# A hybrid encoder trunk: branch pieces go on TensorE only in every second gap between dense products

## The chip, the cores and the metric

The kernel runs on one core of a Trainium2 chip. The metric is the device time of one execution in microseconds; the median of three runs of the kernel before is 1067.63 us.

## What is computed

Two layers of an encoder over 256 tokens of width 1024, all in float32, and a last RMSNorm. Each layer projects the normalised tokens once and feeds four branches from it, merges them through sigmoid gates, and ends with a SwiGLU block. Cut to what matters:

```
h = rms_norm(x); proj = h @ w_in                    # 1024 -> 10000 columns
aq ak av ao ag | bq bk bv | cq ck cv | dq dk dv | gl = split(proj)
y_a = bidirectional mLSTM (4 heads of 128, centred short convolution on q, k)
y_b = grouped-query attention (8 heads of 64, 2 kv heads, rotary)
y_c = neighbourhood attention (8 heads of 64, 8 x 16 window, relative bias)
y_d = softmax(q1 k1' + alibi) v - lambda * softmax(q2 k2' + alibi) v     # 4 heads
merged = sum_g sigmoid(gl_g) * (y_g @ w_up_g);  x += merged @ w_out
h2 = rms_norm(x);  x += (silu(h2 @ w_gate) * (h2 @ w_up)) @ w_down       # 1024 -> 2816 -> 1024
```

## The kernel before

**Dense products.** A float32 product is made of three products of rounded halves, hi x hi, hi x lo and lo x hi (`mm3`, line 354). A weight tile comes by DMA into one of four `raw` buffers; ScalarE (ACT) writes the high half `whi` (`emit_hi`, 255), VectorE (DVE) the low half `wlo` = raw - whi (`emit_lo`, 262), five buffers each. The activations stand as `xT` or `yt`, halves too. Every engine call goes through one line (166), so that the profile's line is the same everywhere, and the tile names tell the work apart: `pd` are the three PSUM banks of the dense products, used in turn (`bank`, 333), `pa` the five banks of the branches.

**What sets the order.** The kernel is a list scheduler written out in the program: the order in which `trunk` issues is the order in each engine's queue. It walks through blocks of dense products (`PLAN`, line 32 and following: d0 d1 dv bkv a0 a1 av bq and so on; then `wo` and the SwiGLU). A block of 512 columns (`blk512`, 368) issues runs of 6 or 12 wide products (128x512), `bkv` (1158) runs of 12 narrow ones (128x272), 6 into `pd1` and 6 into `pd2`. Between two runs it calls `slot` (293): a gap. In each gap, in this order: the evacuations that are due (`later`, 320: the one of a finished bank is issued one gap later), one `emit_lo` on even gaps and one `emit_hi` on odd ones (both if the weights are behind), and then one step of each branch task that is ready.

**The pieces.** The branches are generators: `a_gates`, `a_head`, `soft_item` (one pair of heads of b, c or d), `soft_tail`, `y_up` and others. They run up to their next `yield` in one gap. A piece is a step that puts work on TensorE: transposes (`pa<-ident,...`), score products of 64 rows (`pa<-rq`, 12 of them per item, the two heads in the two halves of the rows), products with the values (`pa<-vd,w` and `pa<-re,...`). A piece starts with a loop that waits for free banks and buffers, as `while not (PS.ok(1) and RE.ok(1)): yield` (917). Between the pieces of an item lie steps without TensorE. In `soft_item` for d these are: the score step on DVE (four `CUSTOM_DVE_ANT_0` with the ALiBi distance, out `w2` and `sm`), four exps on ACT, the normalisation on DVE (a `RECIPROCAL`, then products and sums into `w`), the transposes, a copy, the products with `vd`, a copy into `k4`, two squares on ACT. A product with `vd` or a transpose of `w` is float32 throughout; the products with `vd` stand in the trace as two records each. A step is taken only when by the planner's own durations its operands are ready (`step`, 278).

**The place behind `bkv`.** `bkv` fills `pd1` and `pd2`. Their evacuation `done` (1162) is, for each: `gtok` on DVE, `ktok` and `vb` (high half) on ACT, `vb` (low half) on DVE. It is issued one gap behind the block. The next block `a0` puts its first 6 wide products into `pd0` and the next 6 into `pd1`.

Of the kernel before, what the change touches and what calls it, by code (L numbers as in the profile page):

```python
# [170 lines left out]
def trunk(ctx: ExitStack, tc, x_in, wts, par, parc, cst, dist, t2w, fg, out):  # L171
# [15 lines left out]
    PS = Res([psp.tile([128, 512], F32, name="pa%d" % i, tag="pa%d" % i) for i in range(5)])  # L187
# [9 lines left out]
    RQ = many(2, "rq_", [128, 2, 512], F32R)  # L197
    RE = many(3, "re_", [128, 2, 512], F32R)
# [6 lines left out]
    K4 = many(4, "k4_", [128, 1024])  # L205
    W2 = many(8, "w2_", [128, 512])
# [5 lines left out]
    SM = many(8, "sm_", [128, 16])  # L212
# [17 lines left out]
    with tc.manual_schedule():  # L230

        tasks, urgent, pending = [], [], []
        state = {"load": 0, "hi": 0, "lo": 0, "bank": 0, "u": 0, "live": 0, "n": 0, "dma": 1.5}
        nhalf = 2 * L * NU

        consts = []
# [39 lines left out]
        ready = {}  # L276
# [16 lines left out]
        def slot(forced=False):  # L293

            for r in everyres:
                r.flush()
            now = [p for p in pending if p[0] <= 0]
            pending[:] = [(p[0] - 1, p[1]) for p in pending if p[0] > 0]
            for _, f in now:
                f()  # L300

            if state["u"] <= 2:
                step(urgent, forced)
            if not forced:
                state["n"] += 1
                behind = state["hi"] - state["live"] < NH - 1
                if state["n"] % 2 == 0 or behind:
                    emit_lo()
                if state["n"] % 2 == 1 or behind:
                    emit_hi()  # L310
            if state["u"] > 2:
                step(urgent, forced)
            step(tasks, forced)
# [246 lines left out]
        def y_up(b, y):  # L560
            while not yt_ok(b):
                yield
            yt = yt_get(b)
            for t in (0, 1):
                while not PS.ok(1):
                    yield
                p = PS.get()
                for k in range(4):
                    T.transpose(p[:, k * 128:(k + 1) * 128], y[:, t, k * 128:(k + 1) * 128], ident)
                yield  # L570
                p4 = p.rearrange("p (k n) -> p k n", k=4)
                A.activation(yt[:, 0, :, tsl(t)], p4, AF.Copy)
                yield
                sub_lo(yt[:, 1, :, tsl(t)], p4, yt[:, 0, :, tsl(t)])
                PS.put(p)
            yield
            Bs[b]["yt"] = yt


        def a_gates(res):  # L580

            while not W2.ok(3):
                yield
            w0, w1, w2 = W2.get(), W2.get(), W2.get()
            g = gtok
            g4 = g.rearrange("p (n k h) -> p n k h", k=2, h=4)
            f = w1[:, 32:48]
            V.tensor_copy(f.rearrange("p (n h) -> p n h", h=4), g4[:, :, 1, :])
            for d in (0, 1):
                V.tensor_copy(iz[:, :, 32 * d:32 * d + 4],  # L590
                              g.rearrange("p (t d k h) -> p t d k h", t=2, d=2, k=2)[:, :, d, 0, :])
            mn, ab = w1[:, 48:64], w1[:, 64:80]
            V.tensor_scalar(mn, f, 0.0, None, op0=ALU.min)
            yield
            A.activation(ab, f, AF.Abs)
            A.activation(ab, ab, AF.Exp, scale=-1.0)
            yield
            z, q, pl = w1[:, 80:96], w1[:, 96:112], w1[:, 112:128]
            V.tensor_scalar(z, ab, 2.0, None, op0=ALU.add)
            V.reciprocal(z, z)  # L600
            V.tensor_tensor(z, z, ab, op=ALU.mult)
            V.tensor_tensor(q, z, z, op=ALU.mult)
            V.tensor_scalar(pl, q, 1.0 / 17.0, None, op0=ALU.mult)
            yield
            for n in (15, 13, 11, 9, 7, 5, 3):
                V.scalar_tensor_tensor(pl, pl, 1.0 / n, q, op0=ALU.add, op1=ALU.mult)
                if n == 9:
                    yield
            V.scalar_tensor_tensor(pl, pl, 1.0, z, op0=ALU.add, op1=ALU.mult)
            G.memset(w2[0:36, 0:512], 0.0)  # L610
            G.memset(w0[0:36, 0:512], 0.0)
            yield
            lf = w1[:, 128:144]
            V.scalar_tensor_tensor(lf, pl, -2.0, mn, op0=ALU.mult, op1=ALU.add)
            lf4 = lf.rearrange("p (t d h) -> p t d h", t=2, d=2)
            for d in (0, 1):
                V.tensor_copy(rowz[:, :, d, 32 * d:32 * d + 4], lf4[:, :, d, :])
            yield
            while not PS.ok(1):
                yield  # L620
            p = PS.get()
            tri = cs[:, K_TRI:K_TRI + 384]
            T.matmul(p[0:36, 0:256], rowz[:, 0, 0, :], tri[:, 0:256], start=True, stop=False)
            T.matmul(p[0:36, 0:256], rowz[:, 1, 1, :], tri[:, 128:384], start=False, stop=False)
            T.matmul(p[0:36, 128:256], rowz[:, 1, 0, :], tri[:, 0:128], start=False, stop=False)
            T.matmul(p[0:36, 0:128], rowz[:, 0, 1, :], tri[:, 256:384], start=False, stop=True)
            for t in (0, 1):
                T.transpose(p[0:36, 256 + 128 * t:384 + 128 * t], iz[:, t, :], ident)
            yield

            ar, br = w1[0:36, 0:256], w1[0:36, 256:512]
            A.activation(br, p[0:36, 0:256], AF.Copy)
            yield
            V.tensor_tensor(ar, p[0:36, 256:512], br, op=ALU.subtract)
            PS.put(p)
            V.tensor_scalar(w2[0:36, 128:384], ar, 0.0, None, op0=ALU.max)
            a_, b_ = w2, w0
            for i in range(8):
                d = 1 << i
                V.tensor_tensor(b_[0:4, 128:384], a_[0:4, 128:384], a_[0:4, 128 - d:384 - d], op=ALU.max)  # L640
                V.tensor_tensor(b_[32:36, 128:384], a_[32:36, 128:384], a_[32:36, 128 + d:384 + d], op=ALU.max)
                a_, b_ = b_, a_
                if i % 2 == 1:
                    yield
            m = a_[0:36, 128:384]
            V.tensor_tensor(br, br, m, op=ALU.add)
            A.activation(mrow[0:36, 0, :], m, AF.Copy)
            yield
            A.activation(br, br, AF.Exp, scale=-1.0)
            sub_lo(mrow[0:36, 1, :], m, mrow[0:36, 0, :])  # L650
            yield
            while not PS.ok(1):
                yield
            p = PS.get()
            for t in (0, 1):
                T.transpose(p[:, 36 * t:36 * t + 36], ar[:, tsl(t)], ident[0:36, 0:36])
                T.transpose(p[:, 72 + 36 * t:108 + 36 * t], br[:, tsl(t)], ident[0:36, 0:36])
            yield
            V.tensor_copy(gcols.rearrange("p n t r -> p (n t r)"), p[:, 0:144])
            PS.put(p)  # L660
            W2.put(w0, w1, w2)
            yield
            res["ready"] = True

        def a_head(B, h, pc):

            while not ("t%d" % (h // 2) in B and B["fly"] < 2 and PS.ok(1) and W2.ok(3)):
                yield
            B["fly"] += 1
            tok = B["t%d" % (h // 2)]  # L670
# [26 lines left out]
            V.scalar_tensor_tensor(cv[:, :512], th[:, :512], 1.0, cv[:, :512], op0=ALU.add, op1=ALU.mult)  # L697
            W2.put(xp, th)
            yield
            while not ("v" in B and "ready" in B["g"] and PS.ok(2) and W2.ok(2) and SM.ok(1)):  # L700
                yield
            pS, pM, e0, e1, dn = PS.get(), PS.get(), W2.get(), W2.get(), SM.get()
            for s in (0, 1):
# [21 lines left out]
                V.tensor_tensor(o, o, si, op=ALU.mult)  # L725
            PS.put(pS)
            yield
            while not (PS.ok(2) and ("hb" in B or K4.ok(1))):
                yield
            if "hb" not in B:  # L730
                B["hb"] = K4.get()
# [27 lines left out]
            for t in (0, 1):  # L759
                V.bn_stats(dn[:, 8:14], h4[:, t, h, :])  # L760
                i = t * 4 + h
# [38 lines left out]
        def soft_item(B, i, kind):  # L800


            slope = 4.0 ** (-1 - i) if kind == "d" else 1.0
            while not (B["src"](i) is not None and PS.ok(1) and RQ.ok(1)):
                yield
            qs, ks, free = B["src"](i)
            p, r = PS.get(), RQ.get()
# [5 lines left out]
            n = 256 if ks is None else 512  # L813
# [3 lines left out]
            sub_lo(r[:, 1, :n], p[:, :n], r[:, 0, :n])  # L817
            PS.put(p)
            yield
            while not (PS.ok(2) and W2.ok(2) and SM.ok(1) and B["ready"](i)):  # L820
                yield
            ps, e, sm = (PS.get(), PS.get()), (W2.get(), W2.get()), SM.get()
            for qt in (0, 1):
# [26 lines left out]
            for c in (0, 1):  # L850
                for qt in (0, 1):
                    n = 2 * c + qt
# [29 lines left out]
            SM.put(sm)  # L882
            W2.put(e[1])
            yield
            while not PS.ok(1):
                yield
            p, e0 = PS.get(), e[0]
            for kt in (0, 1):
# [4 lines left out]
            A.activation(e0[:, 0:512], p, AF.Copy)  # L893
            PS.put(p)
            yield
            while not (PS.ok(1) and "v" in B and ("y" in B or K4.ok(1))):
                yield
            if "y" not in B:
                B["yraw"] = K4.get()
# [14 lines left out]

        def soft_tail(B, i, c, e):

            while not (PS.ok(1) and RE.ok(1)):
                yield
            p, r = PS.get(), RE.get()
            for kt in (0, 1):  # L920
# [7 lines left out]
            sub_lo(r[:, 1, :], p, r[:, 0, :])  # L928
            PS.put(p)
            yield  # L930
            while not PS.ok(1):
                yield


# [1 line left out]
            v = [B["v"](kt, i, c) for kt in (0, 1)]  # L936
# [82 lines left out]
        def b_main(B):  # L1019
# [23 lines left out]
            for part in (((k3, 2, 2, 3),), ((q3, 8, 0, 1),)):  # L1043
                for t, (src4, nh, ci, si) in ((0, part[0]), (1, part[0])):
                    src = src4[:, t]
# [12 lines left out]
            yield  # L1058
            V.tensor_scalar(b20, b20, 0.125, None, op0=ALU.mult)
            W2.put(wa, wb, wr)  # L1060
            while not PS.ok(1):
                yield
            p = PS.get()
            for t in (0, 1):
# [494 lines left out]
```

## Time and profile before

| | before |
|---|---|
| median of 3 runs | 1067.63 us (1067.01 to 1068.67) |
| the profiled execution | 1067.73 us, its span 1065.9 us |
| granted clock, mean | 0.998 |
| TensorE (PE) busy | 1054.9 us, 99% |
| VectorE (DVE) busy | 766.9 us, 72% |
| ScalarE (ACT) busy | 617.0 us, 58% |
| GpSimd (POOL) busy | 135.7 us, 13% |
| chain that ended last | PE 91%, DVE 5%, ACT 1%, DMA 1% |

The span is the time from the first to the last instruction in one profiled execution. Busy is the time in which an engine has an instruction under way; TensorE's matmuls overlap, so the spacing of their starts is what one costs. The chain follows the work that ended last back to what released it. PEld is TensorE's loading of weights, which runs beside the products.

### The profile page before, as it was taken

The page shows a single profiled execution, that of the slowest core. Times are in us where ns is not written, and L with a number is a line of the kernel's source. Part 1 is how long each engine was busy: PE and PEld are TensorE (multiplying, and loading weights), DVE is VectorE, ACT ScalarE, POOL GpSimd, SP SyncE. Part 2 cuts the span into 40 slices and gives each one's busy share as a digit, 9 for nine tenths or more (in the row PEclk, how much of TensorE's full clock was granted, in tenths as well). Part 3 has the DMA queues.
Part 4 walks back from the last instruction along what each step waited for, and adds up shares of the span by engine and source line. Part 5 has one row for each costly group of instructions (what it writes and reads, how often), then busy time and mean ns, then how long its engine had stood idle before and what let it go on. Part 6 is the DMA issues. An engine that isn't in the chain of part 4 may idle for free.

```text
span 1065.9 us, 14704 instructions
## 1 busy us (share of the span) xinstructions
PE 1054.9 (99%) x5270; PEld 876.0 (82%) x5270; DVE 766.9 (72%) x1388; ACT 617.0 (58%) x1091; POOL 135.7 (13%) x114
## 2 busy tenths in 40 slices
PE   9999999999999999999999999999999999999997
PEld 7888887888888888888888888888888888888886
DVE  5889799888556755565576989998975766555565
ACT  6766648784445644444468656687744464444443
POOL 0010340143300000000000006214223000000000
PEclk9999999999999999999999999999999999999999
DMA  8355444445555555655644454345365556565552
GB/s 299 124 178 175 157 134 159 155 152 192 183 178 178 191 194 185 200 172 185 199 161 142 162 172 144 133 169 171 136 199 195 178 171 201 182 204 172 198 181 75
DMA packets 53000, 184.80 MB, mean 173 GB/s; under 512 B 6080, under 2 KB 7488, under 8 KB 52928
## 3 DMA queue, kind: packets, MB, share of 16 engines
q1 hardware_dynamic: 50256, 178.33, 49.9%
q10 hardware_dynamic: 2672, 5.55, 1.7%
q8 instruction: 41, 0.67, 0.2%
q14 instruction: 31, 0.25, 0.1%
HBM read 182.80 MB, written 1.05 MB: 172 GB/s over the span
## 4 chain that ended last, share of the span: by engine, by line
PE 91%; DVE 5%; ACT 1%; issue 1%; DMA 1%; POOL 0%; POOLq 0%; ACTq 0%; DVEq 0%
PE pd L166 65%; PE pa L166 26%; DVE w L166 2%; DVE wlo L166 1%; DVE sm L166 1%; ACT w L166 1%; DMA raw<-in_wts_dram 0%; ACT whi L166 0%; DMA x<-in_x_dram 0%; DVE re L166 0%; ACT pa L166 0%; DVE k L166 0%; DVE x L166 0%; ACT k L166 0%; DVE yt L166 0%
## 5 line engine op out<-in xcount | busy, mean ns | idle before, releaser
L166 PE MATMUL pd<-whi,xT 128*128 128x512 f32 (+1 forms) x1952 | 624.3, 391 | 0.0
L166 DVE TENSOR_TENSOR wlo<-raw,whi 128x1024 fp32r<-128x1024 f32 (+2 forms) x344 | 421.4, 1236 | 101.4 <-ACT whi L166 100.1
L166 ACT ACTIVATE whi<-raw 128x1024 fp32r<-128x1024 f32 (+2 forms) x344 | 354.6, 1040 | 140.0 <-PE pd L166 106.4
L166 PEld LDWEIGHTS pd<-whi,xT 128*128 128x128 f32 x1952 | 365.1, 188 | 73.6
L166 PE MATMUL pd<-wlo,xT 128*128 128x512 f32 (+1 forms) x976 | 377.6, 387 | 0.6 <-DVE wlo L166 0.6
L166 PEld LDWEIGHTS pd<-wlo,xT 128*128 128x128 f32 x976 | 183.6, 188 | 35.6 <-DVE wlo L166 1.8
L166 PE MATMUL pa<-whi,yt 128*128 128x512 f32 x408 | 136.8, 397 | 0.0
L166 PEld LDWEIGHTS pa<-whi,yt 128*128 128x128 f32 x408 | 76.6, 188 | 15.5
L166 PE MATMUL pd<-whi,yt 128*128 128x512 f32 (+1 forms) x272 | 86.2, 386 | 0.0
L166 PE MATMUL pa<-wlo,yt 128*128 128x512 f32 x204 | 79.5, 390 | 0.0
L166 DVE SCALAR_TENSOR_TENSOR w<-w,pd 128x256 f32<-128x256 f32 x44 | 18.5, 422 | 83.0 <-ACT w L166 82.8
L166 POOL TENSOR_TENSOR st<-st,mhalf 128x2 f32<-128x2 f32 (+1 forms) x6 | 3.9, 654 | 512.0 <-DVE st L166 512.0
L166 ACT ACTIVATE k<-pd,st 128x512 f32<-128x512 f32 (+1 forms) x52 | 31.5, 624 | 53.3 <-PE pd L166 53.0
L166 PEld LDWEIGHTS pd<-whi,yt 128*128 128x128 f32 x272 | 50.6, 188 | 9.7
L166 ACT ACTIVATE w<-pd,st 128x256 f32<-128x256 f32 (+1 forms) x48 | 23.6, 492 | 51.8 <-PE pd L166 51.8
L166 PE MATMUL pd<-wlo,yt 128*128 128x512 f32 (+1 forms) x136 | 52.2, 384 | 0.0
L166 ACT ACTIVATE yt<-pa 128x512 fp32r<-128x512 f32 x34 | 20.3, 598 | 54.1 <-PE pa L166 54.0
L166 PEld LDWEIGHTS pa<-wlo,yt 128*128 128x128 f32 x204 | 38.4, 188 | 7.3
L166 POOL TENSOR_TENSOR acc<-acc,k 128x512 f32<-128x512 f32 x16 | 31.7, 1982 | 80.6 <-DVE k L166 80.6
L166 DVE TENSOR_TENSOR yt<-pa,yt 128x512 fp32r<-128x512 f32 x30 | 20.7, 690 | 27.1 <-ACT yt L166 27.0
L166 ACT ACTIVATE w<-w,sm 128x256 f32<-128x256 f32 x64 | 31.7, 499 | 13.8 <-DVE sm L166 9.1
L166 PE MATMUL pa<-ident,w 128*128 128x128 f32 (+1 forms) x256 | 36.3, 272 | 0.4 <-DVE w L166 0.3
(156 smaller groups left out, 1017.6 us busy)
## 6 DMA issues: line engine op xcount, KB each, us to landing
raw<-in_wts_dram SPq DMA_DIRECT2D x331, 512.0 KB, 3.8
t<-in_t2w_dram ACTq DMA_DIRECT2D x8, 384.0 KB, 3.5
raw<-in_wts_dram SPq DMA_DIRECT2D x8, 272.0 KB, 3.3
x<-in_x_dram ACTq DMA_DIRECT2D x4, 256.0 KB, 6.1
pt<-in_par_dram SPq DMA_DIRECT2D x1, 584.0 KB, 6.7
pt<-in_par_dram ACTq DMA_DIRECT2D x1, 584.0 KB, 3.8
out_dram<-k SPq DMA_DIRECT2D x2, 288.0 KB, 2.1
raw<-in_wts_dram SPq DMA_DIRECT2D x2, 256.0 KB, 5.0
```

The costliest lines, as they stand in the source:

```text
L166: return f(out, *a, **k)
```

## The change

The state of the scheduler gets a flag `pe`, set at each gap: true on gaps with an even counter (and where a gap is forced, which happens in neither kernel). Thirteen of the loops with which a piece waits for its banks ask for the flag too. So a piece of `y_up`, `a_gates`, `a_head`, `soft_item`, `soft_tail` or `b_main` is issued in even gaps only; their other steps are issued in any gap. The transposes of the layer boundary (`boundary_chunk`), of the merged branches (`mt_chunk`) and of the SwiGLU (`ffn_chunk`) don't ask for it.

```diff
-        state = {"load": 0, "hi": 0, "lo": 0, "bank": 0, "u": 0, "live": 0, "n": 0, "dma": 1.5}
+        state = {"load": 0, "hi": 0, "lo": 0, "bank": 0, "u": 0, "live": 0, "n": 0, "pe": True, "dma": 1.5}
...
             for r in everyres:
                 r.flush()
+
+            state["pe"] = forced or state["n"] % 2 == 0
...
-                while not PS.ok(1):
+                while not (state["pe"] and PS.ok(1)):
...
-            while not (B["src"](i) is not None and PS.ok(1) and RQ.ok(1)):
+            while not (state["pe"] and B["src"](i) is not None and PS.ok(1) and RQ.ok(1)):
...
-            while not (PS.ok(2) and W2.ok(2) and SM.ok(1) and B["ready"](i)):
+            while not (state["pe"] and PS.ok(2) and W2.ok(2) and SM.ok(1) and B["ready"](i)):
...
-            while not (PS.ok(1) and "v" in B and ("y" in B or K4.ok(1))):
+            while not (state["pe"] and PS.ok(1) and "v" in B and ("y" in B or K4.ok(1))):
...
-            while not (PS.ok(1) and RE.ok(1)):
+            while not (state["pe"] and PS.ok(1) and RE.ok(1)):
```

The same two words are added in the other loops (lines 619, 652, 667, 700, 728, 885, 931, 1061; the first pair above is that of line 565). The dense products keep their order and their banks. Runs of pieces between dense products number 153 in the program before and 137 after; the number of pieces is the same.

TensorE at the end of `bkv` in layer 0, before (`vd` are the values of d, `w2` its weights, `ident` a transpose):

```order
L166 MATMUL pd2_63<-whi0_72,xT_82 128x272 x2
L166 MATMUL pd2_63<-wlo0_77,xT_82 128x272
L166 MATMUL pd2_63<-whi0_72,xT_82 128x272
L166 MATMUL pa2_66<-vd_95,w2_3_105 128x128 x4
L166 MATMUL pa0_64<-ident_116,w2_0_102 128x128 x4
L166 MATMUL pd0_61<-whi1_73,xT_82 128x512
L166 MATMUL pd0_61<-wlo1_78,xT_82 128x512
L166 MATMUL pd0_61<-whi1_73,xT_82 128x512 x2
L166 MATMUL pd0_61<-wlo1_78,xT_82 128x512
L166 MATMUL pd0_61<-whi1_73,xT_82 128x512
L166 MATMUL pd1_62<-whi1_73,xT_82 128x512
```

After, at the same place:

```order
L166 MATMUL pd2_63<-whi0_72,xT_82 128x272 x2
L166 MATMUL pd2_63<-wlo0_77,xT_82 128x272
L166 MATMUL pd2_63<-whi0_72,xT_82 128x272
L166 MATMUL pd0_61<-whi1_73,xT_82 128x512
L166 MATMUL pd0_61<-wlo1_78,xT_82 128x512
L166 MATMUL pd0_61<-whi1_73,xT_82 128x512 x2
L166 MATMUL pd0_61<-wlo1_78,xT_82 128x512
L166 MATMUL pd0_61<-whi1_73,xT_82 128x512
L166 MATMUL pd1_62<-whi1_73,xT_82 128x512
```

The 8 pieces between the last narrow and the first wide products are gone from there; `pd1` comes 6 products behind `bkv` in both.

DVE at the same place, before (`ISA` are the score steps, `sm` the sums of an item, `raw`, `whi` and `wlo` the weights):

```order
L166 COPY k4_0_98<-pa3_67 128x2x128
L166 TENSOR_TENSOR wlo1_78<-raw0_111,whi1_73 128x1024
L166 RECIPROCAL sm_5_124<-sm_5_124 128x4
L166 TENSOR_SCALAR sm_5_124<-sm_5_124,sm_0_119 128x2
L166 TENSOR_SCALAR w2_0_102<-w2_0_102,sm_5_124 128x256
L166 SCALAR_TENSOR_TENSOR w2_0_102<-w2_5_107,sm_5_124,w2_0_102 128x256
...
L166 TENSOR_TENSOR wlo2_79<-raw1_112,whi2_74 128x1024
L166 SCALAR_TENSOR_TENSOR gtok_140<-pd1_62,st0_163,pt_136 128x16
L166 SCALAR_TENSOR_TENSOR vb_93<-pd1_62,st0_163,vb_93 128x2x64
```

After:

```order
L166 TENSOR_SCALAR w2_3_105<-w2_3_105,sm_4_123 128x256
L166 SCALAR_TENSOR_TENSOR w2_3_105<-w2_4_106,sm_4_123,w2_3_105 128x256
L166 ISA w2_0_102,sm_5_124<-pa1_65,ndist_69 128x256
L166 ISA sm_5_124 128x1
...
L166 TENSOR_SCALAR sm_5_124<-sm_5_124 128x2
L166 ISA w2_5_107,sm_5_124<-pa2_66,ndist_69 128x256
L166 ISA sm_5_124 128x1
...
L166 TENSOR_SCALAR sm_5_124<-sm_5_124 128x2
L166 SCALAR_TENSOR_TENSOR gtok_140<-pd1_62,st0_163,pt_136 128x16
L166 SCALAR_TENSOR_TENSOR vb_93<-pd1_62,st0_163,vb_93 128x2x64
```

The scores of the second item (`sm_5`) now stand right in front of `gtok`, and behind the normalisation of the first (`sm_4`); before, the normalisation of the second and `wlo2` stood there.

DVE at the end of `bkv` in layer 1, before:

```order
L166 TENSOR_SCALAR sm_7_126<-sm_7_126 128x2
L166 ISA w2_6_108,sm_7_126<-pa4_68,ndist_69 128x256
L166 ISA sm_7_126 128x1
...
L166 TENSOR_SCALAR sm_7_126<-sm_7_126 128x2
L166 TENSOR_TENSOR wlo2_79<-raw3_114,whi2_74 128x1024
L166 SCALAR_TENSOR_TENSOR gtok_140<-pd1_62,st0_163,pt_136 128x16
L166 SCALAR_TENSOR_TENSOR vb_93<-pd1_62,st0_163,vb_93 128x2x64
```

After:

```order
L166 SCALAR_TENSOR_TENSOR w2_1_103<-w2_3_105,sm_7_126,w2_1_103 128x256
L166 TENSOR_TENSOR wlo1_78<-raw2_113,whi1_73 128x1024
L166 RECIPROCAL sm_2_121<-sm_2_121 128x4
L166 TENSOR_SCALAR sm_2_121<-sm_2_121,sm_5_124 128x2
L166 TENSOR_SCALAR w2_7_109<-w2_7_109,sm_2_121 128x256
L166 SCALAR_TENSOR_TENSOR w2_7_109<-w2_4_106,sm_2_121,w2_7_109 128x256
...
L166 TENSOR_TENSOR wlo2_79<-raw3_114,whi2_74 128x1024
L166 SCALAR_TENSOR_TENSOR gtok_140<-pd1_62,st0_163,pt_136 128x16
L166 SCALAR_TENSOR_TENSOR vb_93<-pd1_62,st0_163,vb_93 128x2x64
```

The scores before are replaced by the normalisation of an item (`sm_2`) whose scores went ahead; another one stands just in front of `wlo1`.

## Rows read from the trace of the kernel before

**Rows 1.** The page's first part: busy us (share of the span) and instructions

```profile
PE 1054.9 (99%) x5270; PEld 876.0 (82%) x5270; DVE 766.9 (72%) x1388; ACT 617.0 (58%) x1091; POOL 135.7 (13%) x114
```

**Rows 2.** TensorE's waits: us in total, times, longest us

```profile
PE pa L166 <- DVE re L166: 1.1, 2, 0.6
PE pd L166 <- DVE wlo L166: 0.6, 2, 0.3
...
PE pa L166 <- DVE rq L166: 0.2, 1, 0.2
```

**Rows 3.** Timeline of TensorE: start us, us, engine, operation, out<-in, tile, count

```profile
29.79 1.03 PE L166 MATMUL pa<-ident,acc 128*128 128x128 f32 x8
...
30.90 0.40 PE L166 MATMUL pd<-wlo,xT 128*128 128x512 f32 x1
...
34.85 1.69 PE L166 MATMUL pa<-rq 64*128 64x256 f32 x24
...
36.80 0.40 PE L166 MATMUL pd<-wlo,xT 128*128 128x512 f32 x1
...
37.97 0.60 PE L166 MATMUL pa<-ident,acc 128*128 128x128 f32 x4
...
38.64 0.39 PE L166 MATMUL pd<-wlo,xT 128*128 128x512 f32 x1
...
581.71 0.98 PE L166 MATMUL pa<-rq 64*128 64x256 f32 x12
...
582.95 0.40 PE L166 MATMUL pd<-wlo,xT 128*128 128x512 f32 x1
```

**Rows 4.** Timeline of all engines, 57 to 62 us: end of `bkv`

```profile
57.99 0.23 DVE L166 SCALAR_TENSOR_TENSOR gtok<-pd,st,pt 128x16 f32<-128x16 f32 x1
...
58.91 0.35 DVE L166 SCALAR_TENSOR_TENSOR vb<-pd,st,vb 128x128 fp32r<-128x128 f32 x1 [0.69 <-ACT vb L166]
...
59.53 0.62 PE L166 MATMUL pd<-whi,xT 128*128 128x512 f32 x2
...
60.21 0.62 PE L166 MATMUL pd<-whi,xT 128*128 128x512 f32 x2
```

**Rows 5.** Timeline of DVE, 46 to 66 us

```profile
48.82 0.18 DVE L166 RECIPROCAL sm<-sm 128x4 f32<-128x4 f32 x1 [0.63 <-ACT w L166]
...
50.74 0.42 DVE L166 CUSTOM_DVE_ANT_0 w<-pa,ndist 128x256 f32<-128x256 f32 x1
...
52.51 0.73 DVE L166 TENSOR_TENSOR wlo<-raw,whi 128x544 fp32r<-128x544 f32 x1
...
56.86 1.22 DVE L166 TENSOR_TENSOR wlo<-raw,whi 128x1024 fp32r<-128x1024 f32 x1
```

**Rows 6.** Timeline of TensorE in `bkv`, layer 1 and layer 0

```profile
578.48 0.39 PE L166 MATMUL pd<-whi,xT 128*128 128x272 f32 x1
...
582.61 0.50 PE L166 MATMUL pd<-whi,xT 128*128 128x512 f32 x1
...
50.98 1.95 PE L166 MATMUL pa<-vd,w 128*128 128x128 f32 x16
52.69 0.37 PE L166 MATMUL pd<-whi,xT 128*128 128x272 f32 x1
```

**Rows 7.** The page's costliest groups: count, busy us, mean ns, idle before

```profile
L166 ACT ACTIVATE whi<-raw 128x1024 fp32r<-128x1024 f32 (+2 forms) x344 | 354.6, 1040 | 140.0 <-PE pd L166 106.4
...
L166 ACT ACTIVATE w<-w,sm 128x256 f32<-128x256 f32 x64 | 31.7, 499 | 13.8 <-DVE sm L166 9.1
```

**Rows 8.** TensorE's timeline at the start; windows at the end (us, busy, granted clock)

```profile
1.47 2.51 PE L166 MATMUL pd<-ident 128*128 128x128 f32 x10 [1.47 <-POOL ident masks.py:199]
...
6.50 1.23 PE L166 MATMUL pa<-whi,xT 128*128 128x512 f32 x4
...
1060.00:1061.00 1.00, 0.00 (x0) 0.00 (x0) 0.83 (x4) 0.51 (x2) 0.00 (x0) 1.00 1.02 395
1061.00:1062.00 1.00, 0.00 (x0) 0.00 (x0) 0.39 (x1) 0.39 (x1) 0.55 (x1) 0.67 0.30 113
```

More of the change, by code (lines that the diff above doesn't have):

```diff
@@ L618, in a_gates @@
             yield
-            while not PS.ok(1):
+            while not (state["pe"] and PS.ok(1)):
                 yield
@@ L651, in a_gates @@
             yield
-            while not PS.ok(1):
+            while not (state["pe"] and PS.ok(1)):
                 yield
@@ L665, in a_head @@
         def a_head(B, h, pc):
-            while not ("t%d" % (h // 2) in B and B["fly"] < 2 and PS.ok(1) and W2.ok(3)):
+            while not (state["pe"] and "t%d" % (h // 2) in B and B["fly"] < 2 and PS.ok(1) and W2.ok(3)):
                 yield
@@ L699, in a_head @@
             yield
-            while not ("v" in B and "ready" in B["g"] and PS.ok(2) and W2.ok(2) and SM.ok(1)):
+            while not (state["pe"] and "v" in B and "ready" in B["g"] and PS.ok(2) and W2.ok(2) and SM.ok(1)):
                 yield
@@ L727, in a_head @@
             yield
-            while not (PS.ok(2) and ("hb" in B or K4.ok(1))):
+            while not (state["pe"] and PS.ok(2) and ("hb" in B or K4.ok(1))):
                 yield
@@ L884, in soft_item @@
             yield
-            while not PS.ok(1):
+            while not (state["pe"] and PS.ok(1)):
                 yield
@@ L930, in soft_tail @@
             yield
-            while not PS.ok(1):
+            while not (state["pe"] and PS.ok(1)):
                 yield
@@ L1060, in b_main @@
             W2.put(wa, wb, wr)
-            while not PS.ok(1):
+            while not (state["pe"] and PS.ok(1)):
                 yield
```

## The prediction

> **What bounds the kernel now.** I read the busy times first: TensorE works 1054.9 of the 1065.9 us, DVE 72% [rows 1]. So the time is TensorE's work plus its waits, and a change that moves its work without adding or dropping any can act in two ways only: through waits, and through what it costs TensorE to go from one kind of product to another. The list of TensorE's waits came next. Behind the start its waits come to little, above all 1.1 us for `re` (twice), 0.6 for `wlo` (twice) and 0.2 for `rq` [rows 2]; hardly anything is left to win there. Last I laid the order of the instructions before and after side by side, to find places where little cover stood in front of a bank of dense products; the rows of those places give the rest.
>
> **What the change moves.** The dense products keep their order, banks and number, and the pieces keep theirs; the pieces now stand in every second gap. Stretches of pieces between dense products fall from 153 to 137. A piece whose gap is closed waits for the next one; the generators' other steps (copies, scores, exps) still run in any gap, and so move only as far as their products do. SP's and POOL's work follows those steps; no load is issued later than before relative to the products that need it.
>
> **Fewer switches.** Two stretches of 4 transposes, each with the first dense product behind it, take 2 x 0.67 us (37.97 to 38.64), one stretch of 8 takes 1.11 (29.79 to 30.90) and leaves one more plain dense product of 0.23 [rows 3, 4]: nothing is won. For 64-row pieces (`rq`) it is 2 x 1.24 (581.71 to 582.95) against 1.95 (34.85 to 36.80) plus 0.23: 0.3 us saved where two stretches merge, and about 0.1 of it at each change of kind [rows 3]. By the orders, 17 stretches of 64-row pieces are entered from dense products in both kernels, and 15 are left straight for dense products before, 7 after; the other 8 now run into another piece. 8 x 0.1 = 0.8 us saved is what I take; the bounds are 0 (the change is paid at the next piece as well) and 16 x 0.3 = 4.8 (every stretch that goes is a 64-row one). [...]
>
> **Old waits that go.** Pieces run later in relation to the weights, so `wlo` has less DVE work in front of it at the later of its two waits (0.3), and the waits for `re` (1.1) and `rq` (0.2) get a gap more of cover: 1.6 us [rows 2]. The earlier `wlo` wait stands ahead of the first instruction that differs, and stays. Bounds: 0, and 2.2, if each wait also costs the 0.15 us or so by which the product behind it runs longer.
>
> **A new wait in layer 0.** The orders show one place where cover goes. Behind `bkv`, block `a0` starts: 6 wide products into `pd0`, then `pd1`, which `bkv` filled; its evacuation (DVE `gtok`, ACT `ktok`, ACT `vb`, DVE `vb`) must be through. Before, `pd1` comes free at 58.91 + 0.35 = 59.26, and its first product starts at 60.21 + 0.23 = 60.44 [rows 4]: 1.2 us to spare, with 8 products of pieces standing as cover between `bkv` and `a0`. After, nothing stands there, and on DVE the normalisation of one item and the scores of the next stand before `gtok`.
> I count both queues from the end of the first item's score products. TensorE up to `pd1`: 24 narrow products 3.2 (578.48 to 581.71), 12 score products 0.9 (581.71 to 582.61), 12 narrow 1.6, 6 wide 1.4 (three take 0.68, 59.53 to 60.21) = 7.1 us [rows 3, 4, 6]. DVE up to the free bank: start 0.1, scores 1.8 (50.74 to 52.51), two `wlo` 2.3 (1.13 each, 56.86 to 57.99), normalisation 1.9 (48.82 to 50.74), scores 1.8, evacuation 1.3 (57.99 to 59.26) = 9.1 us [rows 4, 5]. TensorE stands for **2.0 us**. Without the second scores it would be 0.2: they and the normalisation decide. Behind TensorE are then all its dense products, so the wait goes straight into the time.
>
> **The same in layer 1.** Here two items' 24 score products stand just before the last 6 wide products of `dv`, and DVE has two normalisations in place of one and a pair of scores. From the end of those score products, TensorE: 6 wide 1.4, 48 narrow 6.4, 16 records of `vd` 1.7 (50.98 to 52.69), 4 transposes 0.4 (0.67 with a product of 0.23 in it), 6 wide 1.4 = 11.3 [rows 3, 4, 6]. ACT sets when DVE can go on: it holds `vd`'s evacuation until `dv` is done (1.4, and with half a `whi`'s width and the hand-overs 2.3), then half a `whi` 0.6, eight exps at 0.5 and `whi` 1.0, to 7.9 [rows 7]. DVE follows with `wlo` 1.1, normalisation 1.9, `wlo` 1.1, evacuation 1.3 = 13.3 [rows 4, 5]. TensorE stands for **2.0 us**. If ACT weren't in the way, DVE's own work from the score products on would be two scores 3.6, half a `wlo` 0.6 and the 5.4 with the other normalisation, 1.9, = 11.5, and the wait 0.2. So for both layers together the bounds are 0.4 us and, with half a us more of ACT's queue in each, 5; a gain is excluded, since TensorE doesn't wait at these places now.
>
> **Sum**, against the profiled execution (1067.73, of which the span is 1065.9): 1067.7 + 2.0 + 2.0 - 1.6 - 0.8 = 1069.3. It stands 0.1 above the median of the runs, so **1069.2 us**. A measurement of this kernel can tell about 0.2% (2.1 us): the forecast is inside that.
>
> **Rivals.**
> First, *the bank comes free in time*. DVE may be ahead: if the normalisation in layer 0 were through before the sum begins, DVE would need 7.2 against 7.1 and nothing would wait; in layer 1 the same decides, at 2.0 us. For: my DVE durations go from start to start, with small waits in them. Against: they are of the same instructions in the same shapes. Then 1067.6 - 2.2 - 0.8 = 1064.6, faster. Chance 0.14.
> Second, *bunching*, the one that ends slower: what a closed gap held back comes out in the open one, so two items' copies, scores and exps meet on ACT and DVE at once. It decides where they last longer than the two gaps of dense work until the next open one (12 wide products, 2.7 us); two scores (3.5) or four normalisation steps of two items (3.8) do [rows 5]. Then new waits for `re`, `rq` and `w` take the place of the 1.6 us, and the switches bring half: 1067.6 + 4.0 - 0.4 = 1071.2. For: all the waits left now are of this kind [rows 2]. Against: DVE is busy for 72% only [rows 1], and the planner lets a piece go when by its durations the operands are there. Chance 0.26.
> Third, *the clock*. [...] A wait of 2 us in the middle is shown by no row, and the clock might fall in it. The price is bounded by the start, where 22 records take 1.47 to 6.50 = 5.0 us against 2.35 at 0.107 each (1.71 by 16): 2.7 us lost [rows 6, 8], though the granted clock reads 1.00 there. One fall gives 1069.2 + 2.7 = 1071.9, two 1074.6. [...] Chance 0.12.
> That the change doesn't do what it says is excluded by the orders: the 16 stretches are gone.
>
> **How the numbers follow.** The forecast's case has 0.48, with about 1 us to either side; a quarter of it lies beyond 1069.8. Faster: 0.12 of the first rival. Same: 0.36 of the forecast and 0.10 of the others' edges, 0.46. Slower: 0.12 + 0.21 + 0.09 = 0.42. The range reaches from 1065.0 (the waits at their lower bound: 1067.6 + 0.4 - 2.2 - 0.8) to 1072.0 (second rival with its spread, one fall of the clock): about 0.1 is left out on each side.
>
> **What would show it.** In the profile after: two waits of TensorE for a `pd` bank, released by DVE `vb`, near 59 and 585 us, 2 us each (right for both sums); rows for `re` and `rq` shrunk or gone (right for 1.6); new rows for `w`, `re` or `rq` of a us and more (second rival); a granted clock under 1.00 in a slice (third). No wait at `vb` makes the forecast wrong at its main terms; a TensorE busy time that is lower by more than 2 us makes the switches wrong.

## The result

The changed kernel takes 1076.98 us (median of 4 runs, 1075.94 to 1079.27) against 1068.07 before: a ratio of 1.0084 (95% interval 1.0071 to 1.0097). It is 8.9 us slower, where 1.1 us was forecast, and it lies outside the range. The profiled execution of after took 1079.27 us, with a span of 1077.5 us against 1065.9: 11.6 us more, somewhat more than the median shows. The granted clock of the four runs is 0.993 in the two longest (1079.27 and 1077.91 us) and 0.996 and 0.995 in the other two (1076.05 and 1075.94), where the kernel before has 0.998.

The busy times of after, as in [rows 1] (us, share of the span, instructions):

```profile
PE 1059.6 (98%) x5270; PEld 880.1 (82%) x5270; DVE 770.7 (72%) x1388; ACT 618.6 (57%) x1091; POOL 128.7 (12%) x114
```

TensorE has as many instructions as before and is busy 4.7 us longer. Its waits in after, which answer to [rows 2] (us in total, times, longest):

```profile
PE pd L166 <- DVE vb L166: 3.9, 2, 2.1
PE pa L166 <- DVE w L166: 3.7, 3, 1.7
...
PE pd L166 <- DVE wlo L166: 1.2, 1, 1.2
```

The rows for `re` and `rq` are gone and so is the later wait for `wlo`. The first row is the wait for the bank behind `bkv`, once in each layer. The second is new and was in no sum: besides an old wait of 0.4 it has 1.7 us in each layer, where `a_head` multiplies its weights with the values (`pa<-va,w`). The wait for `wlo` stands ahead of the first instruction that differs; in the kernels of this case it was between nothing and 1.8 us there.

The bank wait in layer 0, from the timeline of DVE in after and, below it, that of TensorE, beside [rows 4]:

```profile
57.01 0.17 DVE L166 RECIPROCAL sm<-sm 128x4 f32<-128x4 f32 x1
...
58.93 0.42 DVE L166 CUSTOM_DVE_ANT_0 w<-pa,ndist 128x256 f32<-128x256 f32 x1
...
60.69 0.23 DVE L166 SCALAR_TENSOR_TENSOR gtok<-pd,st,pt 128x16 f32<-128x16 f32 x1
61.61 0.35 DVE L166 SCALAR_TENSOR_TENSOR vb<-pd,st,vb 128x128 fp32r<-128x128 f32 x1 [0.69 <-ACT vb L166]
```

```profile
59.76 0.40 PE L166 MATMUL pd<-whi,xT 128*128 128x512 f32 x1
62.02 0.70 PE L166 MATMUL pd<-whi,xT 128*128 128x512 f32 x1 [1.86 <-DVE vb L166]
```

Normalisation, scores, `gtok`, `vb`: the queue of the prediction, in its order. The bank is free at 61.96, and TensorE has stood for 1.86 us. Now what comes behind that wait, by the windows (us, busy of PE, PEld, DVE, ACT and POOL, granted clock, share of DMA, GB/s):

```profile
61.00:62.00 1.00, 0.00 (x0) 0.00 (x0) 0.39 (x2) 0.58 (x2) 0.00 (x0) 1.00 0.00 0
62.00:63.00 1.00, 0.98 (x3) 0.80 (x4) 0.30 (x2) 0.86 (x3) 0.00 (x0) 0.57 0.00 0
63.00:64.00 1.00, 1.00 (x4) 0.81 (x3) 1.00 (x2) 1.00 (x2) 0.00 (x0) 0.50 0.00 0
64.00:65.00 1.00, 1.00 (x3) 0.80 (x3) 1.00 (x2) 1.00 (x6) 0.00 (x0) 0.50 0.00 0
65.00:66.00 1.00, 1.00 (x5) 0.75 (x3) 0.73 (x5) 1.00 (x5) 0.00 (x0) 0.72 0.57 160
66.00:67.00 1.00, 1.00 (x8) 0.86 (x7) 0.35 (x1) 0.94 (x3) 0.00 (x0) 1.00 0.86 274
```

TensorE works again from 62.02 on, but the granted clock has gone from 1.00 to 0.50. What is missing from 1.00 adds up to 0.43 + 0.50 + 0.50 + 0.28 = 1.7 us of TensorE's work. The same stands behind the head wait in layer 0 (0.50 from 158 to 161 us, again 1.7 us) and the bank wait in layer 1 (0.50 from 595 to 598, 1.7 us); behind the head wait in layer 1 the clock stays at 1.00 (685 to 691). So the 11.6 us between the profiled executions are 3.9 for the bank, 3.4 for `a_head`, 1.0 for the wait ahead of the change, 5.1 for the clock and 0.2 in waits too short for the list, less 1.6 of old waits and 0.4 of TensorE's own work. The profiled execution has three falls; by the granted clocks above, an estimate, the two shorter runs have one or two.

### The profile page after: what moved, and what is told of

Its sections match the earlier page's. It is cut to its first block, busy times and chain, and to the rows that moved or that the text cites. A ratio compares the mean times of both kernels' runs of the same rounds, so it can differ in the third digit from the quotient of the medians.

```text
span 1077.5 us, 14703 instructions
## 1 busy us (share of the span) xinstructions
PE 1059.6 (98%) x5270; PEld 880.1 (82%) x5270; DVE 770.7 (72%) x1388; ACT 618.6 (57%) x1091; POOL 128.7 (12%) x114
## 4 chain that ended last, share of the span: by engine, by line
PE 91%; DVE 5%; ACT 1%; issue 1%; DMA 1%; POOL 0%; POOLq 0%; ACTq 0%
PE pd L166 65%; PE pa L166 26%; DVE w L166 2%; DVE wlo L166 2%; DMA raw<-in_wts_dram 0%; DVE sm L166 0%; ACT w L166 0%; DMA x<-in_x_dram 0%; ACT whi L166 0%; DVE acc L166 0%; ACT pa L166 0%; DVE x L166 0%; DVE st L166 0%; DVE k L166 0%; POOL st L166 0%
## 5 line engine op out<-in xcount | busy, mean ns | idle before, releaser
L166 DVE TENSOR_TENSOR wlo<-raw,whi 128x1024 fp32r<-128x1024 f32 (+2 forms) x344 | 423.0, 1241 | 101.9 <-ACT whi L166 101.0
L166 ACT ACTIVATE w<-pa 64x256 f32<-64x256 f32 (+2 forms) x66 | 26.9, 408 | 21.4 <-PE pa L166 19.7
```

Of the source, the lines that this page charges most:

```text
L166: return f(out, *a, **k)
```

## Experiments

All ratios are to the kernel before, run beside them; its medians there are 1068.05 to 1068.16 us.

**One part undone: `a_head`.** The three loops of `a_head` without the flag:

```diff
-            while not (state["pe"] and "t%d" % (h // 2) in B and ...
+            while not ("t%d" % (h // 2) in B and ...
```

> The changed kernel with the three loops of a_head ungated (the other ten as changed). Theory 'four waits and the clock': the loss of the changed kernel is two waits at bkv's bank (3.9 us), two waits of TensorE for a_head's weights in front of pa<-va,w (3.4 us), and in two or three of the four places a stretch at half clock behind the wait (1.7 us each), less 2 us of old waits and switches that went. Here the two head waits go and the bank waits stay at about 2 us each: 1077.0 - 3.4 - 1.7 to 3.4 = 1070.2 to 1071.9. Rival 'gated gaps cost everywhere' (bunching): another wait of the same kind comes in their place and the time stays above 1074.

1088.84 us, ratio 1.0193 (1.0177 to 1.0208). The waits:

```profile
PE pa L166 <- DVE re L166: 5.5, 5, 2.6
PE pd L166 <- DVE vb L166: 3.9, 2, 2.1
...
PE pa L166 <- ACT re L166: 1.3, 1, 1.3
```

The head waits are gone and the bank waits stay, as my theory had it; the time is a miss, on the rival's side. There are 7.8 us of new waits for `re` and the `sm` behind it, all in two stretches. The first, from TensorE's timeline:

```profile
224.57 0.40 PE L166 MATMUL pd<-whi,xT 128*128 128x512 f32 x1
224.81 1.03 PE L166 MATMUL pa<-ident,w 128*128 128x128 f32 x8
...
229.15 0.73 PE L166 MATMUL pa<-re,vb 128*128 128x256 f32 x4 [1.96 <-DVE re L166]
...
240.24 1.05 PE L166 MATMUL pa<-ident,w 128*128 128x128 f32 x4
240.95 0.66 PE L166 MATMUL pd<-whi,yt 128*128 128x512 f32 x1
```

For 16 us TensorE has pieces alone, one waiting for the other, and what ends it is the first product of b's up block, which needs all of b's output (line 1241 of the kernel before). In this kernel the scheduler has to force its gaps there; in the two kernels compared it never does. A gate that holds pieces back can run into such a deadline. Of the 11.9 us by which this kernel is slower than after, how much is the deadline is asked further down.

**One part undone: d.** `soft_item` without the flag for kind d (`(state["pe"] or kind == "d")` in two loops, no flag in the two that only d has).

> The changed kernel with soft_item ungated for kind d only. The order behind bkv is again that of the kernel before. Theory 'four waits and the clock': both waits for the bank (3.9 us) go with the falls of the clock behind them, the head waits (3.4 us) stay: 1077.0 - 3.9 - 1.7 to 3.4 = 1069.7 to 1071.4. Rival 'gated gaps cost everywhere': the time stays above 1074, with new waits elsewhere. If only the waits counted and the clock not, it would be 1073.1.

1067.28 us, ratio 0.9988 (0.9979 to 0.9998): 2.4 us under the range that was expected. The bank waits went, and the head waits nearly so (0.2 us are left in front of `pa<-va,w`, in layer 1):

```profile
PE pa L166 <- DVE w L166: 0.6, 2, 0.3
PE pa L166 <- DVE re L166: 0.3, 1, 0.3
```

The granted clock is 0.999 on average, with no fall behind a wait. So the head waits aren't the work of `a_head`'s gate alone: they need the gate on d as well.

**The waits filled with work.** In after, at the four waits:

```diff
+                            if order[un.u % NU][1] == "a0" and i == half == t == 0:
+                                fill(PS.free[0], 8)          # 8 products ident x ident
...
+            if h == 2:
+                fill(ps[1], 7)
```

> The changed kernel with useless transposes-sized products (ident x ident into a free branch bank) put on TensorE into the four waits: 8 of them (1.7 us) in front of pd1 at the start of a0, 7 (1.5 us) in front of the first of the two heads' pa<-va,w, in each layer. They do nothing for the result; what TensorE waited it now works. Theory 'the clock': the waits shrink to 0.3 us, the granted clock stays at 1.00, and the two or three falls (1.7 us each) go: 1077.0 - 3.4 to 5.1 = 1071.9 to 1073.6. Rival 'the clock is not what costs': the time stays at 1077 or rises.

1074.01 us, ratio 1.0057 (1.0042 to 1.0072): 3.0 us less than after, with 30 more products on TensorE, and 0.4 above the range of the theory. No wait in front of `pa<-va,w` is left; the only one at the bank, and then the windows behind the place of the first:

```profile
PE pd L166 <- DVE vb L166: 0.3, 1, 0.3
```

```profile
61.00:62.00 1.00, 0.93 (x5) 0.67 (x4) 0.33 (x2) 0.64 (x3) 0.00 (x0) 1.00 0.00 0
62.00:63.00 1.00, 1.00 (x6) 0.79 (x6) 0.98 (x2) 1.00 (x2) 0.00 (x0) 1.00 0.06 16
63.00:64.00 1.00, 1.00 (x6) 0.84 (x5) 1.00 (x2) 1.00 (x5) 0.00 (x0) 1.00 0.00 0
```

The same place, the same time until `pd1` is free, but useless work in place of a wait: the clock stays at 1.00. In the whole of this execution, with a granted clock of 0.999 on average, there is no fall before the end. That the clock's part of the loss comes from TensorE standing still, not from later work being slower for another reason, is shown by this run. One of its four runs took 1076.59 us at a granted clock of 0.997, the others 1073.08 to 1074.35 at 0.998 or 0.999; that a fall stood in that one isn't excluded.

**GpSimd taken away at the head.** The 16 operations with which GpSimd rotates b's queries are left out (b is computed from unrotated queries); the order of the other engines is kept.

> The changed kernel without GpSimd's rotation of the queries (16 operations of b_main, 8 in each layer, are left out, so that branch b is computed from unrotated queries); the order of all other engines is the same. Theory 'GpSimd slows DVE': DVE's operations beside GpSimd's take about twice as long in the changed kernel (a wlo 2.3 us against 1.2), DVE is 3 us late with a_head's weights, and that is the head wait; without GpSimd it falls from 1.7 to under 0.3 us in both layers, 1077.0 - 3.4 - 1.7 to 3.4 = 1070.2 to 1071.9. Rival 'DVE has simply too much work in front': the head waits stay above 1 us each and the time above 1074.

1070.49 us, ratio 1.0020 (1.0011 to 1.0029), as expected. TensorE's waits are 3.9 us for the bank and none for `va,w`. At the place in after, the timelines of DVE, of GpSimd and of TensorE:

```profile
143.23 2.32 DVE L166 TENSOR_TENSOR wlo<-raw,whi 128x1024 fp32r<-128x1024 f32 x1
...
147.32 2.30 DVE L166 TENSOR_TENSOR wlo<-raw,whi 128x1024 fp32r<-128x1024 f32 x1
...
152.81 1.39 DVE L166 SCALAR_TENSOR_TENSOR w<-pa,gcols,mA 128x256 f32<-128x256 f32 x4
...
156.17 1.14 DVE L166 TENSOR_TENSOR w<-w,pa 128x256 f32<-128x256 f32 x4
```

```profile
146.92 3.86 POOL L166 TENSOR_TENSOR k<-k,w 128x512 f32<-128x512 f32 x2
```

```profile
156.64 2.63 PE L166 MATMUL pa<-va,w 128*128 128x129 f32 x12 [1.68 <-DVE w L166]
```

And without the rotation, DVE and TensorE (the lines are one number higher in this kernel):

```profile
143.75 1.23 DVE L167 TENSOR_TENSOR wlo<-raw,whi 128x1024 fp32r<-128x1024 f32 x1 [1.62 <-ACT whi L167]
...
148.16 1.39 DVE L167 SCALAR_TENSOR_TENSOR w<-pa,gcols,mA 128x256 f32<-128x256 f32 x4
...
151.52 1.14 DVE L167 TENSOR_TENSOR w<-w,pa 128x256 f32<-128x256 f32 x4
```

```profile
152.97 1.50 PE L167 MATMUL pa<-va,w 128*128 128x129 f32 x12
```

Beside GpSimd a `wlo` takes 2.3 us on DVE, without it 1.23. DVE comes to `a_head`'s weights at 152.81 against 148.16, 4.65 us later; 1.83 of it is that the whole execution is later there (TensorE's products for this step start at 148.46 and at 146.63), so 2.8 us are DVE's own. TensorE's next piece, released by planned durations that know nothing of this, waits. So the head wait is made of both. In the kernel before, the last head's weights are made in the middle of GpSimd's rotation (`w<-w,pa` at 140.45, the rotation until 145.4). With the gate they come behind the whole of it (156.17, the rotation until 150.8), when DVE is as late as GpSimd has made it.

**What a wait costs by itself.** The kernel before with nine useless DVE operations in front of `gtok`, in each layer:

```diff
+                    if t == 0:
+                        for _ in range(NDUM):          # NDUM = 9
+                            nc.vector.tensor_scalar(scr, pt[:, 0:256], 1.0, None, op0=ALU.mult)
```

> The kernel before, with 9 useless DVE operations of 128x256 put in front of gtok behind bkv, in both layers (some 0.35 us each, 3.2 us; the slack there is 1.2 us). The rest of its order is untouched. It measures what a wait of TensorE of about 2.0 us costs by itself. Theory 'the clock': each wait costs itself and, where the granted clock falls to 0.50 behind it, 1.7 us more: 1068.1 + 4.0 + 1.7 to 3.4 = 1073.8 to 1075.5, with the clock at 0.50 for about 3.4 us behind one or both. Rival 'a wait costs itself': 1072.1, clock 1.00.

1073.36 us, ratio 1.0049 (1.0034 to 1.0064), but this doesn't test the clock as meant. The nine took 2.9 us, so the waits were shorter than planned:

```profile
PE pd L167 <- DVE vb L167: 2.9, 2, 1.5
PE pd L167 <- DVE wlo L167: 2.0, 2, 1.8
...
PE pa L167 <- DVE w L167: 0.8, 2, 0.5
PE pa L167 <- ACT w L167: 0.6, 1, 0.6
```

Behind waits of 1.5 and 1.4 us the clock stayed at 1.00 in this execution. What it does show: a bank wait draws others after it, since DVE and ACT are late as well (0.5 to 0.6 us at each place). Of the 5.2 us, 1.3 remain that these rows don't explain; the execution profiled has 1.5 more than [rows 2] at the start's `wlo`.

**One part alone: d.** The kernel before with the flag on `soft_item` for d only.

> The other way round to ungating d: the kernel before with the gate on soft_item for kind d alone. Theory 'the bank waits are d's': DVE's order behind bkv is that of the changed kernel, two bank waits of 2 us with one or two falls of the clock, old waits for re and rq stay: 1068.1 + 3.9 - 0.3 + 1.7 to 3.4 = 1073.4 to 1075.1, no head wait. Rival 'the head waits come from d's delay as well': waits of 1.7 us in front of pa<-va,w too, 1077 or more.

1075.34 us, ratio 1.0063 (1.0048 to 1.0078), 0.2 above the first theory's range and with the rows that it names: the bank waits are 3.9 us, the clock falls behind both (0.59, 0.50, 0.50, 0.70 from 62 to 66 us), and there is no head wait. One wait for `re` in layer 1 is 1.5 us where it was 0.6.

**`bkv` evacuated a gap earlier.** In after:

```diff
-                                later(lambda t=t: done(t, ps[t]))
+                                later(lambda t=t: done(t, ps[t]), 0)
```

> The changed kernel, all thirteen loops gated, but bkv's evacuation issued in the gap right behind the block instead of one gap later, so that it stands ahead of one piece of DVE work more. By the sums of the prediction, layer 0: DVE is through with its work before TensorE ends bkv, evacuation 1.3 us behind 5.7 = 7.0 against 7.1, no wait; layer 1: 13.3 - 1.1 (one wlo less) = 12.2 against 11.3, 0.9 us. The head waits stay: 1077.0 - 3.1 - 1.7 (one fall less) = about 1072. Rival: what is pushed behind the evacuation (a wlo, the normalisation) makes TensorE wait a gap later as long as before, 1076 to 1077.

1071.07 us, ratio 1.0028 (1.0018 to 1.0038), by the sums of the prediction: no bank wait in layer 0, and in layer 1

```profile
PE pd L166 <- DVE vb L166: 1.0, 1, 1.0
```

where 0.9 was worked out. One of the head waits shrank as well (0.5 in layer 0), so that 1 us more came back than expected.

**The open gaps moved by one.**

```diff
-            state["pe"] = forced or state["n"] % 2 == 0
+            state["pe"] = forced or state["n"] % 2 == 1
```

> The changed kernel with the open gaps moved by one: pieces go on TensorE in odd gaps only, all thirteen loops gated, as many open gaps as before. In layer 0 the second item's scores then stand between bkv and a0 and on DVE behind gtok: no bank wait there. Theory 'it is where a closed gap falls': other waits in other places, the sum of waits behind the start differs from the changed kernel's 9 us by more than 3 us, and the time with it (falls of the clock 1.7 us each behind some of the long ones). Rival 'a closed gap costs as such': the same time, 1075 to 1079.

1067.29 us, ratio 0.9990 (0.9980 to 0.9999). Just as many gaps are closed, and nothing is lost. The largest row of its waits:

```profile
PE pa L166 <- DVE w L166: 2.2, 4, 0.9
```

It has no bank wait in either layer, and no fall of the clock (0.998 on average). The 8.9 us are no price of closing every second gap; they are the price of which gaps are closed at two places in each layer.

**The gate without `a_head` and d.** It stays on `y_up`, `a_gates`, `b_main`, `soft_item` for b and c, and `soft_tail`.

> The changed kernel with a_head and soft_item for d ungated; the gate stays on y_up, a_gates, b_main, soft_item for b and c, and soft_tail. Theory 'each closed gap is harmless where DVE has room': no bank wait, no head wait, and the re waits of the kernel before go: about 1067. Rival 'bunching of b and c beside GpSimd', as seen where a_head alone was ungated (re waits of 8 us in all): above 1075.

1066.13 us, ratio 0.9981 (0.9972 to 0.9990): 2.0 us faster than the kernel before, the best of this case. Its busy times and longest waits behind the start:

```profile
PE 1053.4 (99%) x5270; PEld 875.6 (82%) x5270; DVE 765.4 (72%) x1388; ACT 619.2 (58%) x1091; POOL 135.2 (13%) x114
```

```profile
PE pd L166 <- DVE wlo L166: 0.3, 1, 0.3
PE pa L166 <- DVE w L166: 0.3, 1, 0.3
PE pa L166 <- DVE sm L166: 0.2, 1, 0.2
```

The waits for `re` are gone and TensorE works 1.5 us less [rows 1], with 12 stretches of pieces fewer by the order. That the second comes from the third isn't shown: two executions with the very same order on TensorE, after and the one without the rotation, differ by 1.3 us in TensorE's busy time once the falls are taken off (1054.5 and 1053.1), and the kernel before and the one with useless operations on DVE by 1.4 (1054.9 and 1056.3).

**The gate on `soft_tail` alone**, to find where those 2.0 us are.

> The kernel before with the gate on the two loops of soft_tail alone. Asks where the 2.0 us come from by which the gate on b, c and the rest beats the kernel before. Theory 'the old waits for re': they go with this gate alone (1.1 us), 1068.1 - 1.1 = 1067.0. Rival 'merged score products of b and c': the time stays at 1068, since TensorE's busy time doesn't fall.

1068.86 us, ratio 1.0012 (1.0002 to 1.0022). Neither theory: the waits for `re` halved (0.5 us), but TensorE was busy 1056.0 us, 1.1 more than before, which is no more than two executions of one order differ by. `soft_tail` alone doesn't bring the gain of the kernel above; which of its loops do is left open.

**The planner told of GpSimd.** After, with a DVE operation counted 1.8 times while the planner holds GpSimd busy; and the same in the best kernel.

```diff
+            slow = 1.8 if self.kind == "V" and self.track.pool.until > self.until else 1.0
+            self.until += slow * self.cost(name, out, [out] + reads, k)
```

> The changed kernel, all thirteen loops gated, with one number of the planner changed: a DVE operation counts 1.8 times its duration while by the planner's account GpSimd is still busy. The computation is the same. Theory 'the planner lets a_head's last piece go too early because it doesn't know that GpSimd slows DVE': the head waits (3.4 us) fall under 0.5 us each, the bank waits stay, since GpSimd does nothing there: 1077.0 - 3.4 - 1.7 to 3.4 = 1070.2 to 1071.9. Rival 'the gate leaves no better gap': the head waits stay and the time is 1075 to 1078.

> The kernel with the gate on b, c and the rest, but not on a_head and soft_item for d (1066.1 us), with the planner's number of 1.8 for DVE beside GpSimd. It has no wait over 0.4 us behind the start, so both theories expect little: 1065.5 to 1066.5; 1067 or more if the later pieces lose switches.

1094.97 us, ratio 1.0260 (1.0236 to 1.0284), and 1080.47 us, ratio 1.0119 (1.0104 to 1.0134): both far off. In the first the head waits shrank (under 0.1 us in layer 0, 0.8 in layer 1), but it has

```profile
PE pa L168 <- DVE re L168: 6.7, 6, 1.8
PE pa L168 <- DVE sm L168: 4.2, 4, 1.1
PE pd L168 <- DVE vb L168: 3.9, 2, 2.1
```

Both run into b's deadline: a planner that lets pieces go later has them forced there, and both programs force gaps in front of b's up block in both layers.

**Whose waits are those in front of b's up block?** Two more runs, from the kernel with `a_head` ungated: one without GpSimd's 24 operations for c (c's weights stay unnormalised and its mask is left out), one with the block `ao` moved ahead of b's up blocks.

> The changed kernel with a_head ungated (1088.8 us), without GpSimd's operations for branch c (24 of them: the normalisation of c's weights and the addition of the column mask to its bias table are left out); the order of the other engines is the same. Theory 'GpSimd slows DVE': the waits for re and sm in the b and c region (8 us, with the falls of the clock behind them some 5 us more) fall under 2 us; the bank waits (3.9 us) stay: 1067.6 + 3.9 + 1 to 3.4 = 1072.5 to 1075. Rival 'too much work of DVE and ACT in front of the pieces': the waits for re stay above 5 us and the time above 1080.

1085.92 us, ratio 1.0157 (1.0140 to 1.0174): the first theory falls. The waits for `re` and `sm` are still 6.5 us, only that more of them end on ACT:

```profile
PE pa L167 <- ACT re L167: 3.7, 2, 1.9
PE pa L167 <- DVE sm L167: 1.4, 4, 0.5
PE pa L167 <- DVE re L167: 1.4, 3, 0.5
```

> The changed kernel with a_head ungated (1088.8 us), and the block ao moved ahead of b's two up blocks, so that b's output is needed some 11 us later. Theory 'deadline': the stretch of pieces alone in front of b's up block (16 us, with 4 us of waits in each layer and the falls of the clock behind them) goes; the bank waits (3.9 us) with their falls stay: 1067.6 + 3.9 + 1.7 to 3.4 = 1073.2 to 1074.9. Rival 'DVE and ACT are too slow for b and c as such': waits of 5 us or more for re stay, above 1080.

1080.59 us, ratio 1.0112 (1.0095 to 1.0129), on the rival's side. Of the stretch of 16 us in layer 0, 5.4 remain (226.01 to 231.40), and 8.3 us of the time went with the rest: of the 11.9 us by which ungating `a_head` made after slower, the deadline in front of b's up block is by this run the larger part. Four waits for `re` remain, 7.0 us in all. The longest of each layer (2.4 and 2.3 us) stands in what is left of the stretch: it ends in the first product of `ao`, which asks for two free `w` buffers (line 1198 of the kernel before), and the scheduler forces two gaps there in each layer. So these two come from a deadline as well. What makes the other two, of 1.1 us each, is left open.

## Why the prediction was wrong

**Old waits that go** (1.6 us): right, the four rows named are gone. **Fewer switches** (0.8): not settled. TensorE's busy time less the clock's 5.1 us fell by 0.4 in after and by 1.5 in the best kernel, but two executions of one order differ by 1.3 to 1.4, so no run here separates a saving of this size.

**The new waits in layers 0 and 1** (2.0 and 2.0): 1.86 and 2.07 us. Place, queue and size held. Counted as in the prediction, DVE took 9.1 us in layer 0 (52.86 to 61.96) and 13.3 in layer 1 (some 580.2 to 593.53), both as summed, and ACT held DVE back in layer 1 until 7.9 us as worked out (`wlo` at 588.07). Moving the evacuation a gap earlier changed the waits as the same sums say. Ungating d took them away and gating d alone brought them.

**What failed is the sum behind them, in two terms.** First the clock. I had it as a rival with a chance of 0.12, beside the forecast, though the forecast itself put two waits of 2 us into the kernel; if anything was to make the clock fall, it was those. It was no other case but a consequence of the likeliest one, and should have stood in its sum. With one to two falls at 1.7 us each the same working gives 1070.9 to 1072.6, around the upper end of the range (1072.0). Its price by the start (2.7 us) was my estimate: the granted clock reads 1.00 there, so no run shows that those 2.7 us are the clock's. It was too high; the rows of after give 1.7.

Second the head wait: 3.4 us, with one fall behind it in the profiled execution. It was in no sum; with it the working comes to 1076.0 (1072.6 and 3.4), and with that fall to 1077.7, where 1076.98 was measured. The rival "bunching" had its kind, but not its place nor its cause: I took DVE's durations from rows where DVE works without GpSimd, and looked for long DVE queues behind `bkv` only. [rows 5] could not show it. The timeline of DVE in the kernel before has it:

```profile
138.25 2.28 DVE L166 TENSOR_TENSOR wlo<-raw,whi 128x1024 fp32r<-128x1024 f32 x1 [0.59 <-ACT whi L166]
```

GpSimd works on `k<-k,w` there, from 136.77 on. I didn't walk the order through `a_head` with such durations. By chance nothing waits for that in the kernel before.

Of the signs I named, the waits at `vb`, the shrunk rows and the granted clock came as told; a new row for `w` of a us and more was the one that said the forecast was short.

## What to carry to other kernels

A wait that a change puts on TensorE is to be counted with what follows it: if it is as long as the 1.7 to 2.1 us of this case, set beside the forecast what the clock may take as well. Where a change moves work by a rule, look for the places at which the cover goes, and walk each engine's queue there with the durations that hold when its neighbour is busy (here a `wlo` of 2.3 us beside GpSimd and of 1.23 without it). And a rule that cost 9 us with even gaps cost nothing with odd ones: before it is given up or kept, find the places that decide; here they were two in each layer.

## What the runs showed of the hardware

**The clock falls behind short waits, and not each time.** Seven kernels of this case have the two waits at `bkv` that after has, 1.86 us in layer 0 and 2.07 in layer 1 (3.9 us in all, 2.1 the longest, in each of their lists). In their profiled executions the granted clock fell to 0.50 behind each of the two in five of the seven, and not in the same five: after `a_head` was ungated, for one, it stayed in layer 0 and fell in layer 1, with the planner's number the other way round. None was seen behind the waits of 1.4 and 1.5 us behind `bkv` in the run with useless DVE operations (0.998 on average), nor behind one of 1.5 where d alone was gated (0.995 on average: two falls of 1.7 us in 1074.0 take 0.003 off 0.998). But the length alone doesn't decide: where `ao` was moved ahead, a wait of 2.43 us in layer 0 had no fall behind it and one of 2.3 in layer 1 had, and of the two waits of 1.68 us in front of `pa<-va,w` in after the one in layer 0 had one and the one in layer 1 had none. What decides is left open. The ten falls behind the waits at `bkv` cost 1.7 us each, with some 3.4 us at 0.50; one further on in the kernel with `a_head` ungated, from 767 to 774 us, cost twice that, 3.4 us. A fall stands already behind 1.68 us of standing still. At the end of the kernel before, with nothing left on TensorE, the granted clock is 0.50 from 1062 us on; behind the waits in after it was back at 1.00 after those 3.4 us, in which TensorE worked.

**GpSimd and DVE slow each other.** A `wlo` (128x1024) takes 2.3 us beside GpSimd's `k<-k,w` and 1.23 without it. The other way round, GpSimd in after:

```profile
134.58 0.60 POOL L166 TENSOR_TENSOR w<-ktok,w 128x64 f32<-128x64 f32 x2
...
136.71 1.58 POOL L166 TENSOR_TENSOR w<-ktok,w 128x64 f32<-128x64 f32 x2
```

The second pair began behind a `wlo` that DVE had started at 136.57 and that took its usual 1.26 us; the first had no `wlo` beside it. In these two places it was the one that began later that took longer: the `wlo` at 143.23 began 0.13 us behind an operation of `k<-k,w` and took 2.32 us, while that operation took 1.36; and at 136.71 it was GpSimd, 0.14 us behind a `wlo`. Through what they slow each other is not shown.
